# Moving the first request's embedding gate behind the second request's output projection, and keeping its FFN inner layer in DRAM

## The chip, the cores and the metric

One core of one Trainium2 chip runs the whole kernel. The metric is device time in microseconds, from one launch to its end. TensorE (PE) multiplies, VectorE (DVE), ScalarE (ACT) and GpSimd (POOL) do the element work, SyncE (SP) issues most of the loads; ACT and POOL issue DMAs too.

## What is computed

An encoder layer for two requests with shared weights: P of 512 tokens (4 tiles of 128) and S of 1024 tokens (2 groups of 512). All is float32, width 1024.

```python
u = group_rmsnorm(h, norm_mix_pre);  proj = u @ w_in
# SSD heads and Hyena heads (long convolution) from proj ...
mix = concatenate([y_ssd, y_hy]) @ w_out
h = h + group_rmsnorm(mix, norm_mix_post)
u = group_rmsnorm(h, norm_ffn_pre)
ff = (silu(u @ w_gate) * (u @ w_up)) @ w_down          # inner width 2816 = 22 x 128
h = h + group_rmsnorm(ff, norm_ffn_post)
gate = sigmoid(group_rmsnorm(h, ple_norm_pre) @ w_ple_gate)
h = h + group_rmsnorm(gate * (p @ w_ple_proj), ple_norm_post)
```

## The kernel before

Every float32 product is made of three matmuls (`mm3`, L297: lines 302 to 304), on a high and a low part of each operand; `split_ps` (L325) splits activations on ACT and DVE. Weights come by `load_w` (L261): a 256 KB tile `wst` is loaded by SP, then split into `whi` and `wlo`. `split_w` (L290) does the low part on POOL (L294); while `dma_lo` is set, `split_dma` (L281) copies the negated weight on ACT (L285) and lets a DMA issued by POOL add the weight to it (L286). Each of the three tiles has 6 buffers.

Tile, the scheduling layer, writes each engine's order from the program's order and its own clock; on the chip every engine then runs its list in order. The stretch that the change touches is the last 1600 us:

- **P's FFN** (`ffn`, L1137) stands behind the long convolution of S (`longconv`, L942) in the program, so its matmuls fill TensorE beside that stage. For each of 22 rows `m` it multiplies gate and up (48 matmuls, tile `uh`/`ul`), makes the inner row `mst` (Silu on ACT, product on DVE, L1151, L1152) and splits it into `hh`, `hl`. After rows 3, 6, 9, ... 18 it calls `down` (L1123) for the last three rows, and at the end for four: the down-projection runs in 7 pieces, and each piece ends with 8 additions from PSUM into the accumulators `acc2` (L1132, the first with a copy).
- **The norm chain** behind a GEMM is `post_steps` (L1041): sum of squares, scaling (L1060), residual (L1061), store (L1062), second norm (L334) and 8 transposes per tile (L340).
- `out_group` (L1213) is S's output projection of one token group, a `stream_gemm` (L1161) of two halves of the columns; `half` runs one half beside a norm chain. P's FFN chain goes beside the first half of S's group 0. Then `ple` (L1375) multiplies P's **embedding gate** (192 matmuls of tile `uh`/`ul`), `ple_post` (L1393, at high priority) finishes P, and the second half follows.
- S's **last norm chain**, of token group 1, is rushed (L1341): it has priority. Beside it stand `ple_proj` (L1346) for S, 96 matmuls and 16 transposes, and the first pair of columns of S's gate and up projection. `gate_up` (L1221) works on pairs of columns `m` by a seven-product scheme; its first pair is done for group 0 and for group 1 apart, so its weights are loaded and split twice; the other ten pairs take both groups.

PSUM has two buffers `g` of two banks; `tok_gemm` and a half of `stream_gemm` need both of them.

## Time and profile before

| | us |
|---|---|
| median of 3 runs | 2838.36 (2838.12 to 2838.89) |
| the profiled execution's own time | 2840.43 |
| its span, first to last instruction | 2838.2 |
| TensorE busy in the span | 2687.0 |

The profile counts an engine as busy while an instruction runs; matmuls overlap, so their mean length is more than their pace. A view of waits names who was late for an engine that could not go on. The granted clock is TensorE's, as a share of full speed.

### The profile page before, as it was taken

What the parts mean: (1) busy time and instruction counts of PE and PEld (TensorE: products, weight loads), DVE (VectorE), ACT (ScalarE), POOL (GpSimd) and SP (SyncE); (2) the same over time, 40 slices, a digit from 0 to 9 for tenths busy, and PEclk for the clock granted to TensorE, in tenths of its full rate; (3) what the DMA queues carried; (4) which work ended last, traced back from release to release, by engine and by line L of the source; (5) the groups of instructions that cost most, each with busy time, mean ns of one, the idle gap of its engine ahead of it and who ended that gap; (6) DMA issues with size and microseconds to landing.
All of it is one profiled execution on the core that took longest, in us unless ns stands there. A gap on an engine that the chain in (4) does not pass through costs nothing.

```text
span 2838.2 us, 41732 instructions
## 1 busy us (share of the span) xinstructions
PE 2687.0 (95%) x14696; PEld 2261.8 (80%) x14696; DVE 1763.3 (62%) x2893; ACT 1333.0 (47%) x2580; POOL 1383.5 (49%) x1137
## 2 busy tenths in 40 slices
PE   7999999999999989889999899988799999999998
PEld 5887888778888767668777777776699999987876
DVE  6767996886665897957577726484444344334445
ACT  4434444773234465654444444455533333344453
POOL 4445654443443556535444525555454444455564
PEclk8999999999999999989999999999899999999999
DMA  5645555744344576688988786465632222276755
GB/s 166 184 133 130 142 186 168 223 140 138 108 119 141 166 225 221 208 234 186 216 188 209 189 208 230 160 226 180 170 104 90 83 83 79 88 243 186 240 196 184
DMA packets 448508, 480.05 MB, mean 169 GB/s; under 512 B 29409, under 2 KB 330281, under 8 KB 445995
## 3 DMA queue, kind: packets, MB, share of 16 engines
q1 hardware_dynamic: 340923, 347.34, 40.4%
q0 software_dynamic: 28224, 68.17, 10.8%
q10 hardware_dynamic: 79152, 61.88, 6.9%
q8 instruction: 116, 1.90, 0.3%
q14 instruction: 93, 0.76, 0.1%
HBM read 346.54 MB, written 91.95 MB: 154 GB/s over the span
## 4 chain that ended last, share of the span: by engine, by line
PE 71%; DVE 14%; DMA 5%; issue 4%; POOL 3%; ACT 2%; SPq 0%; POOLq 0%; DVEq 0%; ACTq 0%
PE g L302 18%; PE g L304 18%; PE g L303 18%; PE a L304 3%; PE a L303 3%; PE a L302 3%; PE a L701 1%; DVE W L620 1%; PE a L974 1%; DVE E L616 1%; DVE b L693 1%; POOL wlo L294 1%; PE a L405 1%; DVE ml L327 1%; PE a L629 1%
## 5 line engine op out<-in xcount | busy, mean ns | idle before, releaser
L294 POOL TENSOR_TENSOR wlo<-wst,whi 128x512 fp32r<-128x512 f32 (+1 forms) x544 | 789.7, 1459 | 711.9 <-ACT whi L293 654.8
L293 ACT ACTIVATE whi<-wst 128x512 fp32r<-128x512 f32 (+1 forms) x544 | 339.6, 628 | 490.4 <-PE g L303 336.7
L302 PE MATMUL g<-uh,whi 128*128 128x512 f32 (+1 forms) x1232 | 494.0, 401 | 7.7 <-DVE cv L394 3.6
L304 PE MATMUL g<-uh,wlo 128*128 128x512 f32 (+1 forms) x1232 | 492.6, 400 | 0.0
L303 PE MATMUL g<-ul,whi 128*128 128x512 f32 (+1 forms) x1232 | 491.8, 399 | 0.0
L302 PE MATMUL g<-bh,whi 128*128 128x256 f32 x1056 | 294.1, 284 | 13.7 <-ACT whi L287 5.8
L304 PE MATMUL g<-bh,wlo 128*128 128x256 f32 x1056 | 294.6, 281 | 2.1 <-DMA wlo<-wsum 1.6
L303 PE MATMUL g<-bl,whi 128*128 128x256 f32 x1056 | 295.3, 281 | 0.0
L302 PEld LDWEIGHTS g<-uh,whi 128*128 128x128 f32 x1232 | 233.6, 190 | 67.2 <-issue 8.5
L304 PEld LDWEIGHTS g<-uh,wlo 128*128 128x128 f32 x1232 | 233.1, 189 | 54.1 <-issue 5.8
L303 PEld LDWEIGHTS g<-ul,whi 128*128 128x128 f32 x1232 | 233.4, 189 | 53.5 <-issue 6.9
L327 DVE TENSOR_TENSOR ml<-mx,mh 128x512 fp32r<-128x512 f32 x152 | 141.8, 941 | 183.5 <-ACT mh L326 180.2
L286 POOL DMA_DIRECT2D wlo<-wst x144 | 126.4, 932 | 227.8 <-ACT wlo L285 211.4
L394 DVE SCALAR_TENSOR_TENSOR cv<-g,cols,cv 128x510 f32<-128x510 f32 (+3 forms) x192 | 193.0, 1006 | 64.4 <-ACT cv L388 62.4
L302 PEld LDWEIGHTS g<-bh,whi 128*128 128x128 f32 x1056 | 198.2, 190 | 19.5 <-DVE gt L1228 7.3
L304 PEld LDWEIGHTS g<-bh,wlo 128*128 128x128 f32 x1056 | 200.4, 190 | 2.6 <-DMA wlo<-wsum 1.8
L303 PEld LDWEIGHTS g<-bl,whi 128*128 128x128 f32 x1056 | 200.6, 190 | 0.1
L310 POOL TENSOR_TENSOR rs_t<-rs_t,nhalf 128x1 f32<-128x1 f32 (+2 forms) x112 | 120.8, 1081 | 149.6 <-DVE rs_t L309 146.6
L303 PE MATMUL g<-wlo,uh 128*128 128x264 f32 (+1 forms) x576 | 192.3, 334 | 0.5 <-POOL wlo L294 0.5
L304 PE MATMUL g<-whi,ul 128*128 128x264 f32 (+1 forms) x576 | 191.0, 332 | 1.3 <-DVE rs_t L309 1.3
L302 PE MATMUL g<-whi,uh 128*128 128x264 f32 (+1 forms) x576 | 190.4, 332 | 1.5 <-DVE dt_s L426 0.9
L326 ACT ACTIVATE mh<-mx 128x512 fp32r<-128x512 f32 x152 | 95.8, 630 | 190.8 <-PE g L303 157.3
(334 smaller groups left out, 6114.1 us busy)
## 6 DMA issues: line engine op xcount, KB each, us to landing
wst<-in_w_in SPq DMA_DIRECT2D x192, 256.0 KB
wlo<-wst POOLq DMA_DIRECT2D x144, 256.0 KB, 4.9
wst<-in_w_down SPq DMA_DIRECT2D x132, 256.0 KB
wst<-in_w_out SPq DMA_DIRECT2D x96, 256.0 KB
wst<-in_w_gate SPq DMA_DIRECT2D x92, 256.0 KB
wst<-in_w_up SPq DMA_DIRECT2D x92, 256.0 KB
mx<-hid_s SPq DMA_DIRECT2D x88, 256.0 KB
rw<-rows_s SPq DMA_DIRECT2D x32, 512.0 KB
```

Source lines behind the costliest of these rows:

```text
L286: nc.gpsimd.dma_start(lo, w, accum_op=ALU.add)
L293: nc.scalar.activation(hi, w, AF.Copy)
L294: (eng or nc.gpsimd).tensor_tensor(out=lo, in0=w, in1=hi.bitcast(F32), op=ALU.subtract)
L302: nc.tensor.matmul(ps, lh, rh, start=first, stop=False, skip_group_check=shared)
L303: nc.tensor.matmul(ps, lh, rl, start=False, stop=False, skip_group_check=shared)
L304: nc.tensor.matmul(ps, ll, rh, start=False, stop=last, skip_group_check=shared)
L310: nc.gpsimd.tensor_tensor(out=t[:, :w], in0=t[:, :w], in1=self.nhalf[:, :w], op=ALU.pow)
L326: self.nc.scalar.activation(hi, ps, AF.Copy)
L327: self.nc.vector.tensor_tensor(out=lo, in0=ps, in1=hi.bitcast(F32), op=ALU.subtract)
L394: nc.vector.scalar_tensor_tensor(out[:, a:b], ps[:, a + d:b + d], wcol(w), out[:, a:b], ALU.mult, ALU.add)
L405: nc.tensor.transpose(ps[:, j * 128:(j + 1) * 128], srcs[i + j], self.ident)
L616: nc.vector.scalar_tensor_tensor(E[:, h], rw[:, 0, h], dbf[:, c, gh:gh + 1], rw[:, 1, h], ALU.add, ALU.min)
```

## The change

Two things are done, and a third follows from the second.

1. `ffn` computes all 22 inner rows first and stores each in DRAM (`hid_p`, by ACT). Then one `stream_gemm` over the 22 rows, in PSUM throughout, does the down-projection: for each half of the columns it loads the rows again in pairs (SP, into tile `t`) and splits them (44 splits in place of 22). `down` goes, `mst` has two buffers.
2. P's embedding gate leaves its place beside S's output projection. After P's FFN chain its normalized rows, high and low, are stored in DRAM (`v_p`, 4 stores of 1 MB by ACT). `late_gate` multiplies the gate after S's whole output projection, beside the last norm chain; it loads `v_p` row by row into the tiles `mh`, `ml` (3 buffers each), once for each half of the columns, and stores the sigmoid in DRAM. `late_post` finishes P in four steps beside the pairs of `gate_up`.
3. The first pair of `gate_up` is no longer done for one group at a time.

```diff
+        self.P.v = [tc.dram_tile([8, 128, LP], F32, name=f"v{i}_p") for i in range(2)]
+        self.P.hid = tc.dram_tile([NF, 128, LP], F32, name="hid_p")
...
     def ffn(self, q, g, pool, u):
...
             nc.vector.tensor_tensor(out=t, in0=t, in1=ps[:, 1], op=ALU.mult)
-            hidden.append([self.T(pool, [128, 512], t, F32R) for t in ("hh", "hl")])
-            self.split_ps(t, *hidden[m])
-            if 0 < m < NF - 1 and m % 3 == 0:
-                self.down(pool, acc2, hidden, m - 3, 3)
-        self.down(pool, acc2, hidden, NF - 4, 4)
+            nc.scalar.dma_start(q.hid[m], t)
+
+        def rows(k0):
+            st = self.T(pool, [128, 2, 512], "mx")
+            nc.sync.dma_start(st, q.hid[k0:k0 + 2].rearrange("k p n -> p k n"))
+            out = []
+            for i in range(2):
+                out.append([self.T(pool, [128, 512], t, F32R) for t in ("hh", "hl")])
+                self.split_ps(st[:, i], *out[i])
+            return out
+
+        acc2 = self.new_acc(pool)
+        for _ in self.stream_gemm(rows, NF, I["w_down"][0], self.keep(acc2), wide=False):
+            pass
...
+    def stored(self, pool, src):
+        def rows(k0):
+            out = []
+            for k in range(k0, k0 + 2):
+                out.append([self.T(pool, [128, 512], t, F32R) for t in ("mh", "ml")])
+                for x, part in zip(out[-1], src):
+                    self.nc.sync.dma_start(x.bitcast(F32), part[k])
+            return out
+        return rows
...
+    def late_gate(self, q, pool):
+        def evac(nch, t, ps):
+            sg = self.T(pool, [128, 512], "mx")
+            self.nc.scalar.activation(sg, ps, AF.Sigmoid)
+            self.nc.scalar.dma_start(q.z[t * 128:(t + 1) * 128, nch * 512:(nch + 1) * 512], sg)
+        return self.stream_gemm(self.stored(pool, q.v), 8, self.I["w_ple_gate"][0], evac, wide=False)
...
     def build(self):
...
                 self.half(out, chain)
-                self.ple_post(P, 0, pl, self.ple(P, 0, pl, u))
+                for part, v in zip(u.parts, P.v):
+                    for i, x in enumerate(part):
+                        self.nc.scalar.dma_start(v[i * 4:i * 4 + 4].rearrange("k p n -> p k n"), x.bitcast(F32))
...
                     self.apool = self.pools["m"][0]
+                    for _ in self.late_gate(P, pe):
+                        pass
                     for g in range(2):
                         for _ in self.ple_proj(pe, S, g):
                             pass
-                    both = {0: u0, 1: u1}
-                    self.gate_up(S, [(p, m, {g: both[g] for g in gs}) for p, gs, ms in (
-                        (pe, [0], (0,)), (ph, [1], (0,)), (ph, [0, 1], range(2, NF, 2))) for m in ms], pe)
+                    self.gate_up(S, [(ph, m, {0: u0, 1: u1}) for m in range(0, NF, 2)], pe,
+                                 self.late_post(P, pm))
```

TensorE's list is the same for its first 5013 rows, up to the start of P's FFN, and it has the same number of matmuls of each shape afterwards.

On TensorE in P's FFN, the row at which the gate and up products (`uh`, `ul` as the second operand's source) first give way to the down-projection (`hh`, `hl`). Before, after four inner rows:

```order
L304 MATMUL g_13804<-uh_13265,wlo_13829 128x512
L302 MATMUL g_13804<-uh_13265,whi_13828 128x512
L303 MATMUL g_13804<-ul_13267,whi_13828 128x512
L304 MATMUL g_13804<-uh_13265,wlo_13829 128x512
L302 MATMUL g_13888<-whi_13892,hh_13632 128x512
L303 MATMUL g_13888<-wlo_13893,hh_13632 128x512
```

Now, some 910 rows later in the list, after all 22:

```order
L306 MATMUL g_15252<-uh_13268,wlo_15277 128x512
L304 MATMUL g_15252<-uh_13268,whi_15276 128x512
L305 MATMUL g_15252<-ul_13270,whi_15276 128x512
L306 MATMUL g_15252<-uh_13268,wlo_15277 128x512
L304 MATMUL g_15337<-whi_15351,hh_15341 128x512
L305 MATMUL g_15337<-wlo_15352,hh_15341 128x512
```

Before, such a switch and the switch back stand seven times in the list; now there is one, and all 528 down matmuls follow it, with the last three of eight long-convolution blocks between them.

On TensorE beside the last norm chain (L340 before, L342 now: its transposes, reading `acc`). Before, among the matmuls of S's embedding projection, with its own transposes (L1357, reading `mx`):

```order
L304 MATMUL g_18839<-whi_18835,ml_18754 128x512
L340 MATMUL a_18705<-ident_105,acc_17632 128x128 x4
L340 MATMUL a_18711<-ident_105,acc_17632 128x128 x4
L302 MATMUL g_18858<-whi_18829,mh_18751 128x512
L303 MATMUL g_18858<-wlo_18830,mh_18751 128x512
L304 MATMUL g_18858<-whi_18829,ml_18753 128x512
L302 MATMUL g_18858<-whi_18835,mh_18752 128x512
L303 MATMUL g_18858<-wlo_18836,mh_18752 128x512
L304 MATMUL g_18858<-whi_18835,ml_18754 128x512
L340 MATMUL a_18718<-ident_105,acc_17634 128x128 x4
L340 MATMUL a_18729<-ident_105,acc_17634 128x128 x4
L1357 MATMUL a_18883<-ident_105,mx_18881 128x128 x4
```

Now, among the matmuls of P's gate:

```order
L306 MATMUL g_18471<-whi_18620,ml_18609 128x512
L342 MATMUL a_18424<-ident_108,acc_17351 128x128 x4
L342 MATMUL a_18430<-ident_108,acc_17351 128x128 x4
L304 MATMUL g_18660<-whi_18672,mh_18662 128x512
L305 MATMUL g_18660<-wlo_18673,mh_18662 128x512
L306 MATMUL g_18660<-whi_18672,ml_18663 128x512
L304 MATMUL g_18660<-whi_18672,mh_18662 128x512
L305 MATMUL g_18660<-wlo_18673,mh_18662 128x512
L306 MATMUL g_18660<-whi_18672,ml_18663 128x512
L342 MATMUL a_18437<-ident_108,acc_17353 128x128 x4
L342 MATMUL a_18448<-ident_108,acc_17353 128x128 x4
L304 MATMUL g_18661<-whi_18672,mh_18662 128x512
```

Between the last matmul of S's output projection and the last two transpose rows stand 102 matmuls of the gate and 24 single transposes; the other 90 gate matmuls and S's embedding projection follow them, and after those the first pair of `gate_up`, for both groups at once.

On SP in the same stretch: the loads of the chain's last two residual tiles (`in_x_sample`). Before, behind the weights of the first column pair:

```order
L278 DMA wst_19005<-in_w_gate 128x4x128
L278 DMA wst_19007<-in_w_gate 128x4x128
L278 DMA wst_19009<-in_w_gate 128x4x128
L1051 DMA t_3787_18652<-in_x_sample 128x1024
L1051 DMA t_3794_18693<-in_x_sample 128x1024
L278 DMA wst_19112<-in_w_up 128x4x128
```

Now, behind seven of the sixteen pairs of loads of `v_p`:

```order
L1206 DMA mh_18604<-v_p 128x512
L1206 DMA ml_18605<-v_p 128x512
L1053 DMA t_3748_18371<-in_x_sample 128x1024
L280 DMA wst_18802<-in_w_ple_gate 128x512
L1053 DMA t_3755_18412<-in_x_sample 128x1024
L1206 DMA mh_18608<-v_p 128x512
```

The seventh pair waits for the buffers that the fourth row's matmuls give back, so these two loads cannot be issued before 48 gate matmuls are done.

## Rows read from the trace of the kernel before

**Rows 1.** The page of the profiled execution: the span, and the busy time, share and instruction count of each engine over the whole of it.

```profile
span 2838.2 us, 41732 instructions
PE 2687.0 (95%) x14696; PEld 2261.8 (80%) x14696; DVE 1763.3 (62%) x2893; ACT 1333.0 (47%) x2580; POOL 1383.5 (49%) x1137
```

**Rows 2.** Busy time of each engine in seven stretches. Columns: start and end, length, then busy us (instruction count) of PE, PEld, DVE, ACT and POOL, then the granted TensorE clock as a share of full speed, the DMA engines' mean busy share and GB/s.

```profile
1234.00:1675.00 441.00, 420.41 (x2131) 350.99 (x2132) 279.69 (x457) 207.43 (x354) 194.07 (x156) 0.98 0.84 200
1675.00:1705.00 30.00, 25.22 (x99) 19.60 (x98) 7.84 (x12) 9.53 (x17) 7.33 (x8) 0.89 0.72 210
1760.00:1806.00 46.00, 45.44 (x201) 36.66 (x200) 8.28 (x11) 17.04 (x29) 19.53 (x15) 1.00 0.35 115
1806.00:1860.00 54.00, 46.65 (x188) 35.55 (x187) 36.94 (x28) 22.91 (x42) 32.56 (x26) 0.97 0.66 211
1918.00:1962.00 44.00, 44.00 (x191) 35.49 (x190) 12.86 (x16) 20.48 (x37) 22.89 (x17) 1.00 0.64 186
1962.00:2012.00 50.00, 35.00 (x142) 25.06 (x140) 35.70 (x51) 31.89 (x64) 16.51 (x17) 0.86 0.52 168
2012.00:2092.00 80.00, 67.50 (x504) 64.39 (x505) 37.70 (x50) 43.12 (x85) 45.19 (x39) 0.94 0.62 149
```

**Rows 3.** The waits view of TensorE from 1234 to 1705 us. Columns: who waited (engine, tile, line), for whom, us in total, times, longest.

```profile
PE g L302 <- DVE acc L1132: 9.4, 5, 5.1
PE g L303 <- DMA wlo<-wst: 3.5, 2, 2.7
PE g L302 <- DVE mst L1152: 3.2, 2, 1.9
```

**Rows 4.** The DMA view from 1234 to 1705 us: busy share of the 16 engines in 40 slices (tenths, 9 is 90% or more), then per queue packets, MB and share of 16 engines (q0 is issued by POOL, q1 by SP, q10 by ACT), then one issue group with its count, KB each and median us to landing.

```profile
DMA  2997699769968989779896899699697958779992
...
q0 software_dynamic: 18144, 33.04, 42.1%
q1 hardware_dynamic: 67280, 56.37, 38.5%
q10 hardware_dynamic: 2208, 4.72, 2.8%
wlo<-wst POOLq DMA_DIRECT2D x126, 256.0 KB, 5.1
```

**Rows 5.** The DMA view from 2490 to 2590 us, where SP loads of 2 KB rows are nearly all the traffic: busy share in 40 slices, and the queue of SP.

```profile
DMA  9999999976666666456067877666757766465655
...
q1 hardware_dynamic: 11782, 22.75, 70.7%
```

**Rows 6.** Costliest groups of instructions from 1234 to 1705 us, shapes kept apart, of VectorE. Columns: line, engine, operation, out<-in with shapes, count | busy us, mean ns of one | idle time of the engine just before them and what ended it.

```profile
L1132 DVE TENSOR_TENSOR acc<-acc,g 128x512 f32<-128x512 f32 x46 | 29.5, 680 | 20.8 <-PE g L304 20.8
L327 DVE TENSOR_TENSOR hl<-mst,hh 128x512 fp32r<-128x512 f32 x22 | 16.2, 736 | 5.7 <-ACT hh L326 5.7
```

**Rows 7.** The waits view of TensorE from 1806 to 1860 us (columns as in rows 3).

```profile
PE a L304 <- DVE ml L327: 6.4, 5, 2.8
```

**Rows 8.** The groups of VectorE from 1760 to 1860 us (columns as in rows 6).

```profile
L1388 DVE TENSOR_TENSOR acc<-acc,mst 128x512 f32<-128x512 f32 x8 | 7.6, 951 | 28.0 <-ACT mst L1387 28.0
L1060 DVE SCALAR_TENSOR_TENSOR acc<-acc,rs_t,row 128x1024 f32<-128x1024 f32 x4 | 7.2, 1798 | 0.0
L1061 DVE TENSOR_TENSOR t<-acc,t 128x1024 f32<-128x1024 f32 x4 | 6.9, 1735 | 6.7 <-DMA t<-h_p 6.6
```

**Rows 9.** The waits view of TensorE from 1962 to 2092 us (columns as in rows 3).

```profile
PE g L302 <- ACT mx L1371: 6.4, 4, 4.0
PE g L302 <- ACT whi L287: 5.8, 3, 2.9
PE g L302 <- ACT mh L326: 5.1, 2, 2.8
PE g L304 <- DVE rs_t L309: 3.3, 1, 3.3
```

**Rows 10.** The timeline of TensorE from 1962 to 2013 us. Columns: start us, us, engine, line, operation, out<-in, count [idle before <-releaser]. The first row is the last matmul of the second request's output projection, the L340 rows are the transposes of the norm chain behind it, the last one opens the gate and up projection.

```profile
1962.46 0.40 PE L304 MATMUL g<-whi,ml 128*128 128x512 f32 x1
...
1976.84 1.47 PE L340 MATMUL a<-ident,acc 128*128 128x128 f32 x12
...
1979.78 0.60 PE L340 MATMUL a<-ident,acc 128*128 128x128 f32 x4
...
1990.64 1.07 PE L340 MATMUL a<-ident,acc 128*128 128x128 f32 x8 [0.41 <-DVE acc L334]
...
1994.30 1.06 PE L340 MATMUL a<-ident,acc 128*128 128x128 f32 x8
...
2001.13 0.78 PE L304 MATMUL g<-whi,ml 128*128 128x512 f32 x1
...
2012.58 0.39 PE L302 MATMUL g<-bh,whi 128*128 128x256 f32 x1 [0.69 <-ACT mx L1371]
```

**Rows 11.** The timeline of TensorE from 1884 to 1908 us (columns as in rows 10): first and last transposes of the chain of the second request's first token group, whose GEMM had ended at 1859.8.

```profile
1885.07 1.03 PE L340 MATMUL a<-ident,acc 128*128 128x128 f32 x8
...
1906.34 0.91 PE L340 MATMUL a<-ident,acc 128*128 128x128 f32 x4
```

More of the change, by code (lines that the diff above doesn't have):

```diff
@@ L1121, in new_acc @@
         return [self.T(pool, [128, 1024], tag) for _ in range(4)]
-    def down(self, pool, acc, hidden, m0, cnt):
-        nc = self.nc
-        def evac(nch, t, ps):
-            a = acc[t][:, nch * 512:(nch + 1) * 512]
-            if m0 == 0:
-                nc.scalar.activation(a, ps, AF.Copy)
-            else:
-                nc.vector.tensor_tensor(out=a, in0=a, in1=ps, op=ALU.add)
-        self.tok_gemm(lambda k, t: [x[:, t * 128:(t + 1) * 128] for x in hidden[m0 + k]], cnt,
-                      self.I["w_down"][0], m0 * 128, evac, m0 + cnt == NF)
     def ffn(self, q, g, pool, u):
         nc, I = self.nc, self.I
-        acc2 = self.new_acc(pool)
-        hidden = []
         for m in range(NF):
@@ L1219, in out_post, with gate_up @@
         return u, self.post_steps(pool, acc, "norm_mix_post", q.x, g * 512, q.h1, "norm_ffn_pre", u)
-    def gate_up(self, q, jobs, early):
+    def gate_up(self, q, jobs, early, beside=iter(())):
         nc, I = self.nc, self.I
@@ L1327, in gate_up @@
                 old = p
+            if job is not jobs[0]:
+                next(beside, None)
         for _ in old:
@@ L1396, in ple_post, with late_post, piece @@
                   tags=("bh", "bl", "bl", "bh") if last else ("t4",) * 4)
+    def late_gate(self, q, pool):
[4 more added lines that the diff above has]
+        return self.stream_gemm(self.stored(pool, q.v), 8, self.I["w_ple_gate"][0], evac, wide=False)
+    def late_post(self, q, pool):
+        nc = self.nc
+        def piece(tag, src):
+            x = self.T(pool, [128, 512], tag)
+            nc.sync.dma_start(x, src)
+            return x
+        cols = [slice(c, c + 512) for c in (0, 512)]
+        rw = [piece("ml", self.I["ple_norm_post"][:, c].to_broadcast([128, 512])) for c in cols]
+        for t in range(q.nc):
+            r = slice(t * 128, (t + 1) * 128)
+            ss = [self.T(self.sp, [128, 1], "ss") for _ in cols]
+            junk = self.T(pool, [128, 512], "ml", BF16)
+            es = []
+            for i, c in enumerate(cols):
+                e, sg = piece("mx", q.e[r, c]), piece("mx", q.z[r, c])
+                nc.vector.tensor_tensor(out=e, in0=e, in1=sg, op=ALU.mult)
+                nc.scalar.activation(junk, e, AF.Square, accum_out=ss[i])
+                es.append(e)
+            nc.vector.tensor_tensor(out=ss[0], in0=ss[0], in1=ss[1], op=ALU.add)
+            rs = self.rstd(ss[0], D)
+            for e, w, c in zip(es, rw, cols):
+                h = piece("mh", q.h2[r, c])
+                nc.vector.scalar_tensor_tensor(e, e, rs, w, ALU.mult, ALU.mult)
+                nc.vector.tensor_tensor(out=h, in0=e, in1=h, op=ALU.add)
+                nc.gpsimd.dma_start(q.out[r, c], h)
+            yield
     def build(self):
```

6 lines of the change are left out of this document (3 added, 3 removed).

## The prediction

> **What bounds the kernel now.** The page first [rows 1]: TensorE is busy 2687.0 of 2838.2 us, no other engine over 62%. Its list is the same for its first 5013 rows and holds the same matmuls of each shape afterwards, so the change cannot take work from the bounding engine; it can only move its stalls. So I read the stretches in which its list differs, from 1234 us (start of P's FFN) to 2092 us (from there one pair of gate-and-up columns follows another), then who was late in them, and last what the DMA engines still have free.
>
> The stretches [rows 2] give length less busy time, the idle part, and the clock. P's FFN loses 441 - 420.4 = 20.6 and 30 - 25.2 = 4.8 us, together 25.4; P's gate 0.6; the half projection after it 7.4; the last norm chain 15.0, and the start of gate and up 12.5. Where the granted clock is below 1 TensorE runs for a part of the time at 1.2 GHz in place of 2.4, and what that costs is at most length times the missing share: 441 x 0.02 + 30 x 0.11 = 12 in the FFN, 54 x 0.03 = 1.6, 50 x 0.14 = 7 and 80 x 0.06 = 4.8 in the others. The whole prize is then 61 us idle and up to 25 us of clock, 86 at most. For scale: with nothing late, the 191 matmuls of the stretch from 1918 take 44.0 us [rows 2], 0.230 us each.
>
> **P's FFN.** What goes: six of the seven switches between gate-and-up and down. The waits there [rows 3] are 9.4 us for the additions into the accumulators and 3.2 for the inner row; the last switch keeps about a seventh, so 11 us go, and with them the clock that they cost, in proportion 11 / 25.4 x 12 = 5. Together 16. VectorE loses 48 additions of 0.680 us and gains 22 splits of 0.736 [rows 6], 16 us less work, on an engine that is 63% busy there: nothing. ScalarE issues each inner row's store, waiting for VectorE's product, with the next weight copies queued behind it; it is busy 207 of 441 us [rows 2] and six weight tiles are ahead: nothing.
>
> What comes: DMA traffic. A plain 256 KB load of 2 KB rows costs 0.707 x 100 us / 22.75 MB x 0.262 MB = 0.815 us of all 16 engines [rows 5]; an accumulating one 0.421 x 471 / 126 = 1.57 us [rows 4]. The 22 stores and 22 loads of 512 KB add (22 + 44) x 0.815 = 54 us. The stretch now holds 83.4% of 471 = 393 us [rows 4], so it will hold 447, while TensorE without its stalls needs 471 - 25 = 446. Within it the down phase is tightest: a pair of rows needs two weight tiles and two rows, 2 x (0.815 + 1.57) + 2 x 0.815 = 6.4 us of DMA for 24 x 0.230 = 5.5 us of matmuls. Eleven pairs in two halves, 22 x 0.9 = 20 us short, if a summed share of 1.0 is the limit and nothing was fetched ahead. [...] I take 8: the present stretch reaches nine tenths and more in 19 of its 40 slices [rows 4] and lost 3.5 us on it [rows 3], and the down phase is worse than those slices but has six weight buffers. Net of the FFN: 16 - 8 = **8 us saved**, between -4 and 16.
>
> The Trainium skill, DMA: Bandwidth & Descriptors, section Specifications, gives the 16 engines 435 GB/s together. By that, as an estimate, the same pair (two loads, two accumulations and one load of 512 KB, 1.57 MB) takes 3.6 us and never binds, and the FFN saves its 16. The trace agrees for plain loads only in so far as short stretches come near full use [rows 5]; accumulations move 0.262 MB in 1.57 us, far less.
>
> **P's gate and its norm.** The stretch of the gate itself loses 0.6 us, which move with it. In the half behind it TensorE waits 6.4 us for the low parts of S's rows [rows 7], late because the urgent norm of P holds VectorE: 8 products of 0.951, 4 scalings of 1.798 and 4 additions of 1.735 us [rows 8], 22 us, that now run beside gate and up. But the end of P's FFN chain comes in their place: its last transposes now stand among that half's matmuls, where before they stood among the gate's. I keep half: 0.6 + (7.4 + 1.6) / 2 = **5 us saved**, between 0 and 9. The four 1 MB stores of `v_p` (4 x 4 x 0.815 = 13 us of DMA) lie in a stretch with a share of 0.66: nothing; without that room they would delay the first blocks of S's next norm, which come a half projection later.
>
> **The last norm chain.** Now 130 us, from 1962 to 2092, idle 27.5 and clock up to 11.8, 39 in all. TensorE waits there for ScalarE and VectorE, which serve the rushed chain before the embedding projection's evacuations and splits, and for weight tiles [rows 9]. With the gate in between, the chain's results are asked for later, the projection meets idle engines, and the first pair takes twice the matmuls per weight tile. What stays:
> - The last transposes. They now start 31.8 us after the last output matmul (1962.46 to 1994.30) [rows 10]. In the new list 102 gate matmuls and 24 transposes stand before them, 102 x 0.230 + 24 x 0.11 = 26.1 us (0.11 from 12 transposes in 1.47 us, their length overlapping). The chain is 5.7 us late at its present pace. The group-0 chain, beside a GEMM with POOL splits and without the rush, was at its end 46.5 us after its GEMM (1859.8 to 1906.34) [rows 11]: 20 us late. I take 8, nearer to the rushed chain, since the gate needs no VectorE.
> - The gate's rows from DRAM: three tiles per row, 3 x 0.815 = 2.45 us of DMA for 12 x 0.230 = 2.76 us. With the chain's two loads and four stores of 512 KB, 6 x 1.63 = 9.8, it is 49 us of DMA in 44 us of matmuls: 5 us short at most, nothing at least, since TensorE's wait for the transposes gives the loads time. I take 3.
> - S's embedding projection: its second half, without the chain, took from 2001.13 to 2012.58 for 37 matmuls (8.5 us) [rows 10], 2.9 lost; twice that is 6, or 2 if the chain was still in it.
> - The start of gate and up: 4, between 2 and 8; now 12.5 idle for it.
>
> Sum 8 + 3 + 6 + 4 = 21, so 39 - 21 = **18 us saved**, between 0 (20 + 5 + 6 + 8 = 39) and 29 (6 + 0 + 2 + 2 = 10).
>
> SP's loads of the chain's last two residual tiles now wait for 48 gate matmuls, 11 us after the projection; the transposes that need the first of them came 28 us after it (1990.64) [rows 10]: nothing.
>
> From 2092 on nothing: TensorE's list there is the old one, and P's last steps are 26 loads, 8 stores and 24 VectorE operations of about 0.95 us [rows 8] spread over four column pairs.
>
> **The sum.** 8 + 5 + 18 = 31 us against the execution's own 2840.4: 2809; the median of the runs shown is 2 us below that execution, so **2807 us**.
>
> **Rivals.**
> - *DMA holds up the FFN.* For it: the demand reaches 447 us for 446 of matmuls, and the rows, the weights and the long convolution's loads queue behind each other in SP's one list. If the engines sustain only the 0.834 that they now average, the stretch takes 447 / 0.834 = 536 us, 65 more, and with 23 saved elsewhere the kernel ends at 2807 + 8 + 65 = 2880: slower. It decides from a sustained share below 447 / (471 + 23) = 0.905. Against: nine tenths and more held for whole groups of slices [rows 4, 5]. 10%.
> - *The chain isn't covered.* The gate's loads and POOL splits slow the chain to the pace of group 0, 20 us late, which leaves 39 - (20 + 5 + 6 + 5) = 3 us there, and the FFN saves nothing: 0 + 5 + 3 gives 2830. For it: that chain, too, ran beside a plain GEMM [rows 11]. Against: it had no priority, and VectorE split that GEMM's rows as well. 20%.
> - *DMA does not bind at all*: 16 in the FFN, 5, and 39 - (6 + 0 + 2 + 4) = 27 in the last chain give 2790. For it: the slices at nine leave open how much more would go through, and only 3.5 us were waited for a transfer [rows 3]. 12%. This is what the Trainium skill's rate above would make of it.
> - *The stalls only change places*: each stage that TensorE leaves earlier meets the next one's weights not yet loaded, and the time is 2838. Against: the stretch from 1918 shows a plain stream at full pace with a share of 0.64 [rows 2]. 8%.
>
> **Numbers.** My forecast, about 2794 to 2822, has 50%. The range leaves out the slow rival, half of the third and a part of the fourth: 2788 to 2836. A measurement of this kernel tells 0.2%, 5.7 us, from no change. Faster: 50 + 12 and most (17) of the second rival's 20, 79%; same: 8 + 3, 11%; slower 10%.
>
> **What would show it.** The waits for L1132 gone from the FFN, one short stall at its single switch; the DMA share from P's FFN start to its end near 0.95, and waits of the down matmuls for `wlo` of some 8 us. From the last output matmul to the first S gate-and-up matmul some 80 us (67 + 3 of matmuls and transposes, the rest stalls), TensorE's clock over 0.93 there, waits at the L342 transposes of 5 to 10 us. Wrong would be a down phase over 160 us, a gate over 60 us, or a last chain whose transposes come 45 us after the projection.

## The result and the profile after

The changed kernel takes **2816.77 us** against 2838.45 us for the kernel before on the same chip. That is the median on record of four runs; three of them took 2812.24 to 2818.82 us (median 2814.72), and the fourth ran at a granted clock of 0.555, took 4389.63 us and is left out of every comparison. By the three the ratio is 0.9919, 95% interval 0.9906 to 0.9932: faster by 0.8% or 23 us. The prediction was 2807, range 2788 to 2836. A second measurement gave 2815.28 against 2835.29, ratio 0.9930 (0.9908 to 0.9952). The profiled execution took 2818.82 us.

The head of the page, beside [rows 1]: as many matmuls as before, less time between them. (Line numbers differ by a few between versions: the three matmuls of a product are L302 to L304 before and L304 to L306 in the change.)

```profile
span 2816.7 us, 41918 instructions
...
PE 2672.1 (95%) x14696; PEld 2254.5 (80%) x14696; DVE 1729.8 (61%) x2861; ACT 1327.4 (47%) x2570; POOL 1371.1 (49%) x1127
```

The stretches, as in [rows 2]: the first three are P's FFN, then the two half projections behind it, the late gate with the last norm chain (1906 to 1967), S's embedding projection, and the start of gate and up.

```profile
1232.00:1548.00 316.00, 301.19 (x1539) 254.59 (x1540) 187.36 (x315) 139.52 (x241) 141.05 (x111) 0.97 0.92 221
1548.00:1645.00 97.00, 91.90 (x470) 76.95 (x469) 68.10 (x109) 54.40 (x93) 52.63 (x34) 0.98 0.96 254
1645.00:1707.00 62.00, 53.73 (x224) 42.62 (x223) 12.10 (x19) 30.42 (x54) 17.16 (x18) 0.92 1.03 304
1707.00:1759.00 52.00, 47.51 (x212) 37.53 (x211) 39.39 (x39) 29.58 (x56) 33.11 (x28) 1.00 0.66 213
1759.00:1804.00 45.00, 45.00 (x203) 36.53 (x202) 15.18 (x20) 21.49 (x39) 21.03 (x16) 1.00 0.80 277
1906.00:1967.00 61.00, 51.71 (x230) 39.52 (x229) 37.06 (x42) 34.76 (x63) 37.20 (x30) 0.98 0.85 295
1967.00:2000.00 33.00, 27.05 (x107) 18.81 (x107) 7.84 (x15) 13.62 (x27) 7.64 (x6) 0.94 0.52 172
2000.00:2092.00 92.00, 83.48 (x680) 81.64 (x679) 53.38 (x67) 37.76 (x72) 46.72 (x41) 0.98 0.52 167
```

P's FFN has not gained: 475 us with 316 + 97 + 62 - (301.2 + 91.9 + 53.7) = 28.2 idle, where [rows 2] had 25.4 in 471. The second half projection has no idle time left. TensorE's waits in the FFN, 1232 to 1707 us, beside [rows 3]:

```profile
PE a L703 <- DMA b<-g_s: 14.6, 5, 7.3
PE g L304 <- ACT hh L328: 8.2, 2, 7.9
PE a L995 <- DVE b L978: 3.0, 1, 3.0
```

The additions, the inner row and `wlo` are gone from it. In their place TensorE waits longer for the convolution's blocks, and once, for 7.9 us, for a split inner row. Before, from 1234 to 1705 us, the wait for the blocks was

```profile
PE a L701 <- DMA b<-g_s: 3.2, 2, 1.7
```

The DMA view of the change's stretch, beside [rows 4], sums to a share of 0.94, and a weight's accumulation lands in 6.0 us where it took 5.1:

```profile
q1 hardware_dynamic: 73820, 69.45, 46.3%
q0 software_dynamic: 18144, 33.04, 41.3%
q10 hardware_dynamic: 5376, 10.49, 6.2%
...
wlo<-wst POOLq DMA_DIRECT2D x126, 256.0 KB, 6.0
```

What makes the row late is seen in four timelines of the place: VectorE's last split out of the buffer that the reload needs, SP's issues from 1658 us, then ScalarE's split of the row, then the matmul that waits for it.

```profile
1660.77 0.69 DVE L329 TENSOR_TENSOR hl<-t,hh 128x512 fp32r<-128x512 f32 x1 [0.87 <-ACT hh L328]
```

```profile
1658.36 0.38 SPq L1143 DMA_DIRECT2D t<-hid_p  x1
1660.49 3.07 SPq L1192 DMA_DIRECT2D mx<-mix_s  x4
...
1667.08 1.01 SPq L1053 DMA_DIRECT2D t<-in_x_sample  x2
1669.21 0.38 SPq L1143 DMA_DIRECT2D t<-hid_p  x1
```

```profile
1681.87 1.15 ACT L328 ACTIVATE hh<-t 128x512 fp32r<-128x512 f32 x2 [8.46 <-DMA t<-hid_p]
```

```profile
1682.55 1.22 PE L304 MATMUL g<-whi,hh 128*128 128x512 f32 x2 [7.92 <-ACT hh L328]
```

The buffer is free at 1661.46, yet the reload of the pair is issued at 1669.21, 7.7 us later, behind four loads of rows and two residuals for the next projection; its split starts 12.7 us after that. In the second profile of the change these two are 7.3 and 13.1 us.

In the last chain the waits of TensorE, from 1906 to 2000 and from 2000 to 2092 us, beside [rows 9], are led by one that the prediction has no term for: the transposes of the embedding rows wait for their load.

```profile
PE a L1367 <- DMA mx<-in_p_sample: 7.1, 3, 5.1
PE g L304 <- ACT mx L1381: 2.5, 3, 1.2
PE g L304 <- DMA mh<-v_p: 2.1, 3, 1.0
...
PE a L342 <- DVE acc L336: 1.1, 2, 0.9
```

```profile
PE g L304 <- DVE gt L1236: 3.1, 3, 1.4
PE a L304 <- ACT whi L295: 2.6, 1, 2.6
PE g L304 <- ACT sc L1275: 2.2, 2, 1.2
```

Lengths of the stages, from the start of the first matmul of each in the timeline, in us; two numbers are two profiles. The last three columns are experiments below.

| stage | before | change | late gate alone | new FFN alone | gate at its old place |
|---|---|---|---|---|---|
| up to P's FFN (same code in all) | 1234.1, 1231.4 | 1232.2, 1228.8 | 1229.3 | 1225.7 | 1229.2 |
| P's FFN | 471.1, 470.0 | 474.9, 466.4 | 480.1 | 468.6 | 473.8 |
| first half projection | 54.5, 54.5 | 52.1, 52.3 | 54.5 | 52.6 | 52.1 |
| P's gate, where it is | 46.2, 46.2 | | | 47.0 | 47.0 |
| second half projection | 53.9, 51.0 | 44.7, 44.7 | 44.5 | 49.4 | 43.3 |
| S's second group | 102.9, 102.7 | 102.9, 103.1 | 103.6 | 102.9 | 104.5 |
| last output matmul to end of gate and up (the late gate in it) | 517.9, 515.7 | 552.4, 551.3 | 555.1 | 517.1 | 512.9 |
| rest | 357.6, 357.5 | 357.6, 357.6 | 357.6 | 355.9 | 358.0 |

The first line has the same code in every column and spans 8.4 us, so a difference of a few microseconds in one pair of profiles is no finding. On the means of two and two the FFN's stretch changed by nothing (470.6 and 470.6), the first half projection by -2.3, the second by -7.7, and the gate with the last chain by 563.0 - 551.9 = -11.1: together -21.

### The profile page after: what moved, and what is told of

It reads as the page before. It is cut to its first block, busy times and chain, and to the rows that moved or that the text cites. A ratio compares the mean times of both kernels' runs of the same rounds, so it can differ in the third digit from the quotient of the medians.

```text
span 2816.7 us, 41918 instructions
## 1 busy us (share of the span) xinstructions
PE 2672.1 (95%) x14696; PEld 2254.5 (80%) x14696; DVE 1729.8 (61%) x2861; ACT 1327.4 (47%) x2570; POOL 1371.1 (49%) x1127
## 4 chain that ended last, share of the span: by engine, by line
PE 70%; DVE 11%; DMA 10%; issue 4%; POOL 2%; ACT 2%; SPq 1%; POOLq 0%; DVEq 0%; ACTq 0%
PE g L304 17%; PE g L306 17%; PE g L305 17%; PE a L304 3%; PE a L305 3%; PE a L306 3%; PE a L703 2%; DMA b<-g_s 1%; DMA wlo<-wst 1%; DVE E L618 1%; DVE W L622 1%; PE a L407 1%; PE a L976 1%; PE a L631 1%; PE a L595 1%
## 5 line engine op out<-in xcount | busy, mean ns | idle before, releaser
L296 POOL TENSOR_TENSOR wlo<-wst,whi 128x512 fp32r<-128x512 f32 (+1 forms) x546 | 778.4, 1431 | 745.4 <-ACT whi L295 668.3
L304 PE MATMUL g<-uh,whi 128*128 128x512 f32 (+1 forms) x1232 | 493.3, 401 | 5.9 <-DVE cv L396 4.0
L306 PE MATMUL g<-uh,wlo 128*128 128x512 f32 (+1 forms) x1232 | 491.8, 399 | 0.0
L304 PE MATMUL g<-bh,whi 128*128 128x256 f32 x1056 | 292.2, 282 | 10.4 <-DVE gt L1236 6.1
L306 PE MATMUL g<-bh,wlo 128*128 128x256 f32 x1056 | 293.1, 280 | 0.0
L304 PEld LDWEIGHTS g<-uh,whi 128*128 128x128 f32 x1232 | 233.4, 189 | 65.3 <-issue 10.2
L306 PEld LDWEIGHTS g<-uh,wlo 128*128 128x128 f32 x1232 | 232.7, 189 | 53.9 <-issue 5.8
L329 DVE TENSOR_TENSOR ml<-mx,mh 128x512 fp32r<-128x512 f32 x152 | 133.5, 882 | 200.6 <-ACT mh L328 189.2
L288 POOL DMA_DIRECT2D wlo<-wst x132 | 116.5, 938 | 219.3 <-ACT wlo L287 188.1
L304 PEld LDWEIGHTS g<-bh,whi 128*128 128x128 f32 x1056 | 197.2, 189 | 15.1 <-DVE gt L1236 8.5
L312 POOL TENSOR_TENSOR rs_t<-rs_t,nhalf 128x1 f32<-128x1 f32 (+2 forms) x112 | 128.1, 1146 | 150.0 <-DVE rs_t L311 148.2
L304 PE MATMUL g<-whi,mh 128*128 128x512 f32 x476 | 192.3, 404 | 7.9 <-ACT mx L1381 2.5
L306 PEld LDWEIGHTS g<-bh,wlo 128*128 128x128 f32 x1056 | 199.4, 189 | 0.0
L306 PE MATMUL g<-whi,ml 128*128 128x512 f32 x476 | 185.3, 402 | 11.9 <-DVE ml L329 11.5
L305 PE MATMUL g<-wlo,mh 128*128 128x512 f32 x476 | 190.0, 399 | 0.0
```

Source lines behind the costliest of these rows:

```text
L288: nc.gpsimd.dma_start(lo, w, accum_op=ALU.add)
L296: (eng or nc.gpsimd).tensor_tensor(out=lo, in0=w, in1=hi.bitcast(F32), op=ALU.subtract)
L304: nc.tensor.matmul(ps, lh, rh, start=first, stop=False, skip_group_check=shared)
L305: nc.tensor.matmul(ps, lh, rl, start=False, stop=False, skip_group_check=shared)
L306: nc.tensor.matmul(ps, ll, rh, start=False, stop=last, skip_group_check=shared)
L312: nc.gpsimd.tensor_tensor(out=t[:, :w], in0=t[:, :w], in1=self.nhalf[:, :w], op=ALU.pow)
```

## The experiments

Theory: the FFN's switches are gone, but the reloads of the inner rows into nearly full DMA engines make other transfers late; the gains come from VectorE's urgent norm and from the cover of the last chain. Rivals: the new FFN saves nothing or costs time by itself; the lateness comes from the splits or the order of a queue; the half projection was slow for another reason than the norm.

**The two halves of the change apart.** The first kernel keeps the old `down` and `ffn` and has the late gate; the second has the new `ffn` and the gate at its old place.

```diff
 first kernel, against the change:
...
-            nc.scalar.dma_start(q.hid[m], t)
...
+            hidden.append([self.T(pool, [128, 512], t, F32R) for t in ("hh", "hl")])
+            self.split_ps(t, *hidden[m])
+            if 0 < m < NF - 1 and m % 3 == 0:
+                self.down(pool, acc2, hidden, m - 3, 3)
...
 second kernel, against the kernel before: the new ffn with its one-piece down-projection and two mst buffers, and
+        self.P.hid = tc.dram_tile([NF, 128, LP], F32, name="hid_p")
...
```

> The gate's move alone: P's FFN as in the kernel before (seven down pieces from SBUF, no inner rows in DRAM), gate and last norm of P as in the change. If the FFN's part of the change gained nothing because the DMA engines are full there: the FFN stretch is 471 us again in place of the change's 475, the output projections and the last chain keep the change's savings (13.5 and 10 us), total 2813, the same as the change or 4 us below it. If the DRAM inner layer itself gave the gain, the total goes back towards 2830 or more.

> The FFN's part alone: inner rows in DRAM and the down-projection in one piece, but P's embedding gate and its norm at the old place and the first gate-up pair group by group, as before. If the DMA engines are the limit of that stretch: FFN stretch 475 us, total 2840 to 2843, nothing gained. If the removed switches had been worth the 8 us of the forecast and the change's FFN is only slow because of what comes behind it: total 2830.

Measured: the late gate alone 2823.81 us against 2836.27, ratio 0.9953 (0.9937 to 0.9969), 12 us saved; the new FFN alone 2827.28, ratio 0.9967 (0.9955 to 0.9978), 9 us saved. The two add up to the change (0.47 + 0.33 = 0.80%). Read from one pair of profiles, the gate had been given all of the gain and the FFN a loss; the times give each its part, the gate some 10 us less than expected and the FFN a gain. That gain lies less in the FFN's own stretch, which took 468.6 us against 471.1 and 470.0, than behind it: the first half projection 52.6 against 54.5, the second 49.4 against 53.9 and 51.0. With the late gate and the old FFN the first half stays at 54.5. There the first transposes of P's chain wait, in the old FFN alone, for VectorE; this is the waits view of 1709 to 1764 us of the late gate alone:

```profile
PE a L342 <- DVE acc L336: 3.4, 1, 3.4
```

The row stands with the same 3.4 us in both profiles of before and in none with the new FFN. It was not the last block's additions that held VectorE: before, the last of them ended at 1706.6, and VectorE sat idle for 1.15 us after them. It was one scaling of the norm, beside five weight splits in a row on POOL (timelines of VectorE and POOL, before):

```profile
1715.46 6.58 DVE L1060 SCALAR_TENSOR_TENSOR acc<-acc,rs_t,row 128x1024 f32<-128x1024 f32 x1
1715.93 7.24 POOL L294 TENSOR_TENSOR wlo<-wst,whi 128x512 fp32r<-128x512 f32 x5
```

A scaling of the same shape took 1.29 us at 1713.06, and this one 6.58 again in the other two profiles with the old FFN; in the nine with the new FFN beside the convolution no VectorE instruction of the place takes over 3.6 us. So the new FFN shifts which norm step meets POOL's splits; that this is why the first half is shorter fits all twelve profiles, but no run changed the order alone.

**Down weights split on POOL.** The accumulating DMA is left for a subtraction on POOL in the down-projection.

```diff
         acc2 = self.new_acc(pool)
+        self.dma_lo = False
...
```

> The change, but the down-projection's 44 weight tiles get their low part by a POOL subtraction in place of an accumulating DMA, which takes 44 x 1.57 = 69 us of DMA out of the tightest part. If full DMA engines make the down phase wait (theory 1): the waits of the down matmuls for the splits of reloaded rows (8.2 us) go, the DMA share after the gate-up rows falls from 0.96 to 1.03 down to about 0.6, total 2803 to 2809. If the reloaded rows' extra splits on ScalarE and VectorE, or the order of SP's list, cause them (theory 2): the waits stay, total 2817. If POOL then delays the long convolution: above 2817.

Measured: 2819.71 us, ratio 0.9936 (0.9918 to 0.9955), no gain. The profile is that of the slowest of its four runs, 2829.57. The down phase's DMA share fell from 0.99 to 0.58, and it took 167.1 us instead of 158.7. Its waits (1552 to 1719 us) have gone over to VectorE, whose 128x1024 product in L760, one of several of that shape, took 1.63 us on the mean of this FFN instead of 1.22. The stretch, then its waits:

```profile
1552.00:1719.10 167.10, 149.13 (x689) 121.61 (x688) 118.32 (x138) 66.61 (x109) 102.47 (x55) 0.95 0.58 195
```

```profile
PE g L306 <- DVE hl L329: 6.6, 4, 3.6
PE a L976 <- DVE b L760: 4.3, 1, 4.3
PE a L995 <- DVE b L978: 4.2, 1, 4.2
```

**Every fourth weight tile split on POOL**, through the whole FFN.

```diff
+        self.tiles = 0
...
-            hi, lo = self.split_dma(st) if self.dma_lo else self.split_w(st)
+            self.tiles += self.dma_lo
+            hi, lo = self.split_dma(st) if self.dma_lo and self.tiles % 4 else self.split_w(st)
```

> The change with every fourth weight tile of the FFN split by a subtraction on POOL in place of the accumulating DMA: some 31 of 126 accumulations go, 31 x 1.57 = 49 us of the DMA engines' work in 475 us, so the share falls from 0.94 to about 0.84, the value before the change. Theory A (it is the fullness of the DMA engines that makes the convolution's blocks late): the waits for b<-g_s fall from 14.6 to 3 to 6 us, the value that they had with the old FFN, the hh wait under 3, and the time is 8 to 12 us below the change. Rival (POOL's subtractions slow VectorE, as when all the down-projection's tiles were split there: its down phase took 167 us): the waits move to VectorE's products and splits, and the time is within 4 us of the change.

Measured: 2814.98 us, ratio 0.9937 (0.9918 to 0.9955); the change on the same chip 2815.28. Both theories were half right. The gate-and-up phase, 1232 to 1547 us, and TensorE's waits in it (lines here are two further down than in the change):

```profile
1232.00:1547.00 315.00, 302.68 (x1541) 254.84 (x1540) 207.49 (x305) 127.64 (x219) 148.23 (x110) 0.98 0.80 204
```

```profile
PE a L978 <- DVE b L762: 7.2, 4, 4.4
PE a L978 <- DVE b L794: 4.0, 4, 1.4
PE a L705 <- DMA b<-g_s: 1.1, 1, 1.1
```

With the share down from 0.92 to 0.80 the wait for the convolution's blocks all but went (14.6 and 7.1 in the two profiles of the change, 1.1 here). That the traffic had made them late is the likely reading; but 11 us came back as waits for VectorE in the same convolution, and a TensorE held up there also gives the next block's load more time, which this run doesn't tell apart. The share alone doesn't set that wait: with the same gate-and-up code it was 5.4 us at 0.94 (the run without reloads, below) and 14.6 at 0.88 (the run before this one). The product that was slowed and that TensorE waits for, first in the change, then here; another of the same shape, L966, took 1.49 us there and 1.35 here:

```profile
L760 DVE TENSOR_TENSOR b<-K 128x1024 f32<-128x1024 f32 x16 | 18.9, 1220 | 13.7 <-POOL K L968 13.7
```

```profile
L762 DVE TENSOR_TENSOR b<-K 128x1024 f32<-128x1024 f32 x16 | 27.3, 1745 | 14.7 <-POOL K L970 14.7
```

**No reloads in the second column half.**

```diff
+        loaded = []
...
-            st = self.T(pool, [128, 2, 512], "mx")
-            nc.sync.dma_start(st, q.hid[k0:k0 + 2].rearrange("k p n -> p k n"))
+            if len(loaded) < NF // 2:
+                st = self.T(pool, [128, 2, 512], "mx")
+                nc.sync.dma_start(st, q.hid[k0:k0 + 2].rearrange("k p n -> p k n"))
+                loaded.append(st)
+            st = loaded[-1]
...
```

> The change without the 11 reloads of the second column half: it splits the last loaded pair of rows again each time, so ScalarE and VectorE do the same work, and the output is that of wrong rows. It takes 11 x 1.63 = 18 us of all 16 DMA engines out of the down-projection's second half, where the share was 1.03. Theory A (the full DMA engines make the inner rows and the convolution's blocks late there): the wait of 8 us for hh goes, the down phase (159 us) becomes 149 to 153, the time falls by 6 to 9 us against the change. Rival (the rows are late because their splits queue on ScalarE and VectorE behind other work): the hh wait stays at 5 us or more and the time within 2 us of the change.

The kernel leaves out 11 of the 22 loads, so its second column half is made of the wrong rows: a probe, and no version to use. Measured: 2799.85 us, ratio 0.9892 (0.9865 to 0.9918), 15 us below the change on the same chip by the medians and 12 by the means, about twice what was expected. In the profile the FFN takes 454.6 us and its down phase 148.3 against 159.1; no wait for `hh` is left in it, and the granted clock is 0.99 instead of 0.96:

```profile
1228.00:1534.00 306.00, 300.33 (x1538) 253.99 (x1539) 187.08 (x315) 139.70 (x241) 140.80 (x111) 0.98 0.94 228
1534.00:1683.00 149.00, 142.92 (x692) 118.11 (x692) 81.86 (x128) 85.49 (x149) 70.54 (x54) 0.99 0.94 250
```

ScalarE and VectorE do as many splits as in the change, so the splits are not the cause. What is worth seeing is that the share has hardly fallen, 0.94 in place of 0.97 to 0.99: the stall goes though the engines have hardly more room. That fits a stall for one late transfer, of which none is left here.

**Four reloads less, the others in another order**, with a complete result.

```diff
+        order = list(range(0, NF, 2))
+        again = order[-2:] + order[-3::-1]
...
+            if k0 in held:
+                return held.pop(k0)
+            if k0 in raw:
+                st = raw.pop(k0)
+            elif k0 < 4:
+                st = raw[k0] = [acc2[k0 + i][:, 512:] for i in range(2)]
...
```

> The change with the second column half of the down-projection in another order of rows: it begins with the last two pairs, whose split rows are still there, goes back from the ninth pair to the third, and ends with the first two, which lie in the half of the accumulators that is written last. Four of the 11 reloads go (4 x 1.63 = 6.5 us of all 16 DMA engines), above all the two at the end, where one reload came 8 us late. The result is complete. Theory A (the second half's reloads are what the full DMA engines make late; without all 11 the time fell by 15 us and the down phase from 159 to 148): the hh wait of 7 to 8 us is under 3, the down phase 150 to 154, the time 5 to 10 us below the change, a ratio to before of 0.989 to 0.991. Rival (the 15 us came from taking all the traffic away, and the stall moves to the next late reload): the hh wait stays at 5 us or more, the ratio 0.992 to 0.993.

Measured: 2816.13 us, ratio 0.9932 (0.9917 to 0.9946): it comes out on the rival's side, by a narrow margin in the wait (5 us or more was asked for). The down phase took 155.7 us, and its waits (1549 to 1705 us) begin with

```profile
PE g L304 <- ACT hh L328: 4.8, 1, 4.8
```

The last two reloads are gone, and another, issued at 1667.96 behind five loads for the next projection and two weight tiles, is split at 1680.97, 13.0 us later. Its buffer had been free for only 1.9 us, where the change's late reload had waited 7.7, so here the time to landing makes the stall, and not the place in the list. That the stall goes to whichever reload meets the prefetch is argued from these timelines; no run moved the prefetch itself.

**More buffers for the reloads**, alone and with the next experiment's buffers.

```diff
-            st = self.T(pool, [128, 2, 512], "mx")
+            st = self.T(pool, [128, 2, 512], "hr")
...
-                pl |= tags(tp, ("acc", 4), ("mst", 2), ("row", 2), ("junk", 1))
+                pl |= tags(tp, ("hr", 4), ("acc", 4), ("mst", 2), ("row", 2), ("junk", 1))
```

> The change with four buffers of their own for the reloaded pairs of inner rows, where they share two with the chain's tiles: the reloads run up to four pairs ahead of the splits. Theory A (the stall of 8 us at the end of the down-projection is one reload that is issued late, behind the next stage's loads, into full DMA engines): the hh wait falls under 2 us, the down phase from 159 to about 151, and the time 5 to 9 us below the change, a ratio to before near 0.990. Rival (the engines are full whatever the order, so the same stall appears at another transfer): the hh wait goes, a wait for wlo or for the next rows of 4 us or more takes its place, and the ratio stays at 0.992 to 0.993.

> The same with the late gate's sigmoid in buffers of its own as well, which by itself gave 0.9916: the wait of 7 us for the embedding rows goes, and one of some 7 us for the gate's evacuations came in its place in that profile. Theory A: 5 to 9 us below that version, 2801 to 2806 if before is at 2836 there. Rival: no better than it, 2808 to 2813.

Measured: 3118.49 us, ratio 1.1002 (1.0985 to 1.1019), and 3127.55, ratio 1.1032 (1.1017 to 1.1047). Neither theory had this. The list of TensorE is another: the second request's convolution no longer runs beside P's FFN but ahead of it, by itself. The two stretches, first the convolution, then the FFN:

```profile
1300.00:1650.00 350.00, 167.77 (x807) 146.56 (x808) 189.42 (x284) 72.94 (x110) 112.10 (x64) 0.71 0.32 106
1650.00:2000.00 350.00, 350.00 (x1529) 284.35 (x1528) 45.30 (x66) 181.91 (x325) 109.92 (x128) 1.00 1.00 238
```

The buffers take 16 KB of each partition; that the convolution's own buffers then no longer fit beside them is the likely reason, and was not tried apart. As a test of the late reload the run tells nothing. It tells something else: without the convolution beside it the FFN runs for 350 us at a share of 1.00 without one idle moment of TensorE.

**The late gate's sigmoid in buffers of its own.**

```diff
-            sg = self.T(pool, [128, 512], "mx")
+            sg = self.T(pool, [128, 512], "sg")
...
-                    for _ in self.late_gate(P, pe):
+                    for _ in self.late_gate(P, pe | {"sg": ph["gt"]}):
```

> The change, but the late gate's sigmoid goes into six buffers of its own instead of the four that S's embedding inputs need next. If the embedding's transposes waited 7.1 us for their inputs because those loads stood behind the sigmoid's stores for a buffer: that wait goes, total 2810 to 2812. If the loads were late because the DMA engines are busy with the gate's rows: the wait stays, total 2817.

Measured: 2810.46 us, ratio 0.9916 (0.9896 to 0.9936), not to be told from the change. The wait for the embedding rows fell from 7.1 to 1.6 us, as meant. But the program's order shifted, the chain's last 16 transposes stand together ahead of the gate's second half, and in the waits of 1903 to 2002 us two others have come for it. The profile is that of the slowest of the four runs, 2820.39; the other three took 2810 to 2811, so these waits need not stand in them:

```profile
PE g L304 <- ACT gt L1412: 7.5, 1, 7.5
PE a L342 <- DVE acc L336: 3.9, 2, 3.4
```

**The gate's GEMM at its old place, its norm and product late.**

```diff
...
-                for part, v in zip(u.parts, P.v):
-                    for i, x in enumerate(part):
-                        self.nc.scalar.dma_start(v[i * 4:i * 4 + 4].rearrange("k p n -> p k n"), x.bitcast(F32))
+                self.old_place_gate(P, pl, u)
...
-                    for _ in self.late_gate(P, pe):
-                        pass
```

> The gate's GEMM back at its old place, with its sigmoid stored to DRAM, and only the norm and the product behind it (ple_post) moved beside gate and up. Theory A (the second half projection of S's first group was slowed by VectorE's urgent norm of P alone): that half takes 45 us here as in the change (53.9 before, 44.7 after). The last norm chain loses its cover and costs what it did before, 10 us more than in the change: time 8 to 11 us above the change. Rival (the half was slowed by what stands around it, the gate's place included): 50 us or more in that half and 14 us or more above the change.

Measured: 2817.12 us, ratio 0.9945 (0.9929 to 0.9961), 2 us above the change by the medians, 4 by the ratios, within the noise. The second half took 43.3 us without an idle moment, with the gate's matmuls ahead of it as before, so it was P's urgent product and norm that had slowed it:

```profile
1802.00:1845.00 43.00, 43.00 (x187) 34.66 (x186) 10.19 (x14) 18.35 (x33) 22.89 (x18) 1.00 0.64 203
```

The cover of the last chain is worth less than expected by time, 8 us by the profiles: gate and last chain took 47.0 + 512.9 = 559.9 us here, 551.9 in the change, 563.0 before. The chain by itself, uncovered, runs as in [rows 2]:

```profile
1950.00:2001.00 51.00, 35.05 (x139) 24.72 (x137) 40.41 (x57) 32.38 (x63) 22.68 (x20) 0.83 0.50 175
```

**Both kernels once more**, for second profiles.

> The change itself once more, for a second profile and for its time on the chip of the three kernels beside it. Between the profiles of the six kernels so far, stretches with the same code differ by some us (everything before the request's FFN took 1225.7 to 1234.1 us), so the FFN's length in one profile (471 before, 475 after; 480 with the old FFN and the late gate, 469 with the new FFN alone) decides nothing by itself. Theory A (the new FFN saves 8 to 10 us, as the times of the two halves of the change say): the FFN's stretch comes out below 475 here, near 470. Theory B (it saves nothing, its full DMA engines take back what the switches gave): 475 or more. The median in both cases 2812 to 2818.

> The kernel before once more, for a second profile of its stretches. The old FFN took 471 us in its first profile and 480 with the late gate beside it; the new one 466 to 475 in five profiles. Theory A (the new FFN itself saves 4 us or so, the rest of its 9 lies in the two half projections behind it): 473 to 480 here, the first half projection 54 to 55, gate and second half together 99 to 101, from the last output matmul to the end of gate and up 517 to 519. Theory B (the FFN's stretch saves nothing): 468 to 472.

Measured: the change 2815.28 us, FFN 466.4; the kernel before 2831.18 in one run, FFN 470.0, first half projection 54.5, gate and second half 97.2, last chain 515.7. On the FFN's stretch this is theory B's side for before and theory A's for the change: it took 470 to 480 us with the old FFN in three profiles, 466 to 475 with the new one in five (means 473.7 and 471.4), a gain too small to be told from the scatter. Theory A's other figures for before were missed: gate and second half 97.2 where it had 99 to 101, the last chain 515.7 where it had 517 to 519. No complete version that was run beats the change by more than the measurement tells.

## Why the prediction was right in sum and wrong in a step

- **The sum**: 31 us predicted, 23 measured; 2807 against 2816.77. The forecast's own mechanisms carry it: the stalls moved, TensorE's work stayed, nothing changed behind gate and up (357.6 us in both). By part it is less good: 8, 5 and 18 were predicted and 0, 10 and 11 measured, so two parts that were too high are made up in part by one that was too low, and that is luck.
- **P's FFN, 8 predicted, in its stretch 0 (2 on the means of all profiles): the failed step is the price of the DMA traffic.** The removed stalls went as told: the rows for L1132 (9.4) and the inner row (3.2) are absent, and of the one switch that stays no wait is seen. The traffic was to cost 8 us, on `wlo` in the down phase. The total share was foreseen (0.95 predicted, 0.94 measured), its effect was not. In the down phase the reloads of one column half alone cost 10.6 us (158.9, the mean of the change's two profiles, to 148.3). Where I had no term, the convolution's blocks were waited for 14.6 and 7.1 us in gate and up where it was 3.2 and 2.5 before; over the whole FFN it is 5.4 to 15.7 in all eight profiles with accumulations throughout gate and up, and 2.5 to 6.3 in the three of the old FFN. That makes 15 to 22, about the 20 of a full shortfall, and it took all that the switches gave. The error was to price a full DMA system by the engines' time, as a rate that is short of the demand. The runs show that a share doesn't tell the price (1.00 without a stall beside no convolution, 0.94 with no row waited for in the run without reloads). What they show in its place is single transfers that land late and are needed soon, 12.7 us for one pair of rows; how much of that is the order of SP's list and how much the full engines stays open.
- That the traffic could cost nothing, which gives the 16 us at the upper end for the FFN, no run shows. POOL's accumulating packets took 0.175 us each before (0.421 x 471 x 16 / 18144) and 0.173 in the change, so what the engines hold grew with the demand.
- The Trainium skill, DMA: Bandwidth & Descriptors, section Specifications, with its 435 GB/s would have seen no bound in the FFN. The trace does not bear that out: in the stretch with the 7.9 us stall the engines' time was full, a share of 1.03, at 304 GB/s.
- **What the new FFN saved**: 9 us by the times of that half alone. In its profile 2 lie in the FFN's stretch, within the scatter, 1.9 in the first half projection and 3.1 in the second (49.4 with the gate at its old place). The forecast looked for its worth in the FFN alone. The 16 us less work of VectorE, costed at nothing, are not shown to be what gave it: the first half's 2.3 us go with a scaling that no longer meets five of POOL's splits, and the second half's part was not traced.
- **P's gate and its norm, 5 predicted, 7.7 in the second half projection** (2.3 more in the first). The half-and-half was too careful: its premise that the chain's transposes would slow that half proved harmless. Three groups of four (1767 to 1781 us) stand there, and the stretch has 45.00 us busy of 45.
- **The last norm chain, 18 predicted, 11 measured.** Idle there is 61 - 51.7 + 33 - 27.1 + 92 - 83.5 = 23.7 us, and the clock costs up to 61 x 0.02 + 33 x 0.06 + 92 x 0.02 = 5; 21 in all had been left. The transposes, given 8, wait 1.1: the chain was faster than the pace that I took from [rows 11]. The loads of the gate's rows, given 3, cost 2.1. The embedding projection, given 6, waits 2.5 for its evacuations and 7.1 for its rows, because `in_p` is loaded into the `mx` buffers that the gate's sigmoid holds until its store is done (with buffers of its own the wait was 1.6): a wait that the change adds, and that I had not looked for. Gate and up, given 4, is idle 8.5.
- **The rivals**: DMA that holds up the FFN to 2880 did not come; its mark, a sustained share of 0.905, was passed (0.94), and the FFN got no longer, as the slices at nine tenths had let expect. The uncovered chain at 2830 did not come. DMA that doesn't bind at all is refuted by the run without reloads. That the stalls only change places is true of the FFN's own stretch, and in the last chain of the new wait for `in_p`.
- The signs named ahead: the L1132 waits gone, the share and the clock over 0.93 held; the `wlo` wait in the down phase was an `hh` wait, of that very size, 8.2, by chance; from the last output matmul to gate and up it was 93 us instead of 80.

## What to carry to other kernels

Work that is spilled to DRAM to spare a stall must be priced by the transfers that TensorE waits for: list which loads stand in the same queue around each reload, above all the next stage's prefetch, and ask which of them is needed first; a mean DMA share says little. When work moves between engines, look at the stage behind too: which of its steps now run side by side on VectorE and POOL. When a step is moved, ask whose buffers its outputs hold. Differences of a few microseconds between stages of two single profiles need a second profile of each before they are explained.

## What the runs showed of the hardware

- A DMA share of 1.00 over 350 us (four buffers for the reloads) went with a TensorE that was busy for all 350 of them at full clock. A summed share can exceed one: 1.03 over 62 us.
- The accumulating DMA landed later at the higher share: 5.1 us at 0.83, 6.0 at 0.94; a packet of it took 0.175 and 0.173 us, so the packets themselves were no longer. From the issue of a 512 KB reload in the fullest stretch to its split it took 12.7 us.
- One 128x1024 product of VectorE (L760) took 1.22 us with the weights' low parts made by DMA and 1.75 with a quarter of them made on POOL, so that work taken from the DMA engines came back as VectorE's. A 128x1024 scaling took 6.58 us beside five splits in a row on POOL, and 1.29 just before.
- Taking 16 KB of each partition for four buffers cost 300 us, and the order of the program was another: the granted clock was 0.71 in the stretch where the convolution ran alone with TensorE 48% busy.
